# A two-layer encoder trunk: normed chunks one group earlier, and three kinds of steps on another engine

## The chip, the cores and the metric

The kernel runs on one core of a Trainium2 chip. Its time is the device time of one launch in microseconds (us), from the first instruction to the last with the little that lies around them. Beside the times there is one profiled execution, which records every instruction of each engine: PE (TensorE: matmuls; PEld is its weight load), DVE (VectorE), ACT (ScalarE), POOL (GpSimd) and SP (SyncE, which issues the DMAs). The granted clock of TensorE is recorded too, as a share of full speed.

## What is computed

A trunk of two layers over 272 rows: 256 tokens and 16 learned meta rows, 2048 features wide, in float32. For each layer, cut to what matters:

```
proj = h @ w_in                                   # 2048 x 6176: GLA q,k,v,r, decay; NA q,k,v
g    = log_sigmoid(decay @ w_up + b_up) / 16      # gates of the gated linear attention (GLA)
# GLA, both directions: scores[t,s] = sum_d q[t,d] k[s,d] exp(b[t,d] - b[s,d]),  b = cumsum(g)
# NA: each token attends to a window of its 64-wide grid, and to the meta rows
h = layer_norm(alpha*h + concat(gla*silu(r), na) @ w_out) * ln1_w + ln1_b
h = layer_norm(alpha*h + square(relu(h @ w_ff1)) @ w_ff2) * ln2_w + ln2_b
```

`w_ff1` is 2048 x 8192. The meta rows are dropped at the end, so that the last layer works on 256 rows from its output projection on (n = 256; elsewhere n = 272).

## The kernel before

**Matmuls.** Activations lie transposed: 16 chunks (DC) of 128 features x n rows. A float32 product is made of three float32r products: each operand is split into a high part (rounded to float32r) and a low part (what is left), and high·high, high·low and low·high are summed. A weight tile is 128 x 1024 numbers, that is eight blocks of 128 x 128. `weights` (L118) loads it (`raw`, a DMA that SP issues), ScalarE makes the high part `wh` (L126) and VectorE the low part `wl` (L127); three tiles of each are in flight. `three` (L130) does one block: with n = 256 the high weight part meets both halves of the activation in one matmul of 512 columns (L135) and the low part makes a second (L136); otherwise there are three matmuls (L139 to L141).

Output columns come in groups of 512, eight weight tiles each. `by_m` (L169) makes a group's four 128-column outputs one after the other, each in a PSUM bank of its own, from two weight tiles. `by_k` (L152) keeps four banks open and takes the activation chunks in pairs, a weight tile for each pair, so that it can begin before all chunks are there (L165).

**What sets the order.** The rest of the work (evictions, attention, norms) is written as generators in two queues, `fg` and `bg`. `pump` (L102) steps them between weight tiles by the credits it is given, `drain` empties them. The framework's planner then orders the instructions of each engine by priority and by costs of its own; a step is issued behind the last `wl` made (`issue_after(self.wl)` in `step`). Each engine works through its own list in order.

**Behind a norm.** `ln_norm` (L796) makes mean and variance. `ln_all` (L816) then goes through the chunks in pairs: VectorE subtracts the mean and multiplies with 1/sigma over two chunks at once (`ln_wide`, L833), and GpSimd applies gain and bias to each of the two (L823). `renew` (L835) splits a normed chunk anew into high and low (L186, L187). TensorE can't wait for this. So the first two groups behind a norm use chunks that aren't normed, with gain multiplied in and two extra columns at their end (n+2), and `fix` (L848) corrects the outputs after: it copies the two columns' sums (`wb`, L857), and takes mean and 1/sigma into account (`fx`, L858 and L859). Group 0 is by_m with `pump=(1, NORMS)`, NORMS = 0.4, which steps `ln_all` now and then; group 1 is by_k with `renew` called at each pair, which makes `ln_all` go on where it has not yet done the chunk. From group 2 on the chunks are normed ones. There are three such places: FF1 in either layer, and in layer 1 the first two projection groups (`win[0]`, `win[1]`).

**Gate differences.** GLA's decays between two positions are made level by level: at each of eight levels (`operands`, L424) the running sums of gates `be` (forward and backward direction) are subtracted from one of their own entries in the middle of each block, for the query and the key side: four GpSimd subtractions (L437), then exp on ScalarE (L442) and the product with q and k on VectorE (L443). Four heads, two layers: 64 levels.

**Residual parts.** In `mixed` (L260, the add is L266) GpSimd adds the high and low part of each old chunk to get the residual back, 16 chunks in each layer.

Of the kernel before, what the change touches and what calls it, by code (L numbers as in the profile page):

```python
# [34 lines left out]
GLA_R, GLA_NA, NORMS = 1.3, 1.1, 0.4  # L35
# [11 lines left out]
class Trunk:  # L47
    def __init__(self, ctx, tc, ins, out):
        self.ctx, self.tc, self.nc = ctx, tc, tc.nc
        self.i, self.out = ins, out  # L50
        self.bg, self.fg, self.credit, self.fcredit = deque(), deque(), 0, 0
        self.x = [None] * DC
        pool = lambda name, **k: ctx.enter_context(tc.tile_pool(name=name, **k))
        self.cp = pool("const", bufs=1)
        self.xp = pool("xhl", bufs=1)
        self.yp = pool("yhl", bufs=1)
        self.wp = pool("wst", bufs=3)
        self.jp = pool("jn", bufs=1)
        self.pm = pool("pm", bufs=4, space=PSUM)
        self.pb = pool("pb", bufs=4, space=PSUM)  # L60
# [57 lines left out]
    def weights(self, ap, parts=1):  # L118
        nc = self.nc
        size = ap.shape[-1]  # L120
        raw, wh, wl = (self.wp.tile([P, WB], d, name=nm, tag=nm)[:, :size]
                       for nm, d in (("raw", F32), ("wh", F32R), ("wl", F32R)))
        for p in range(parts):
            c = slice(p * size // parts, (p + 1) * size // parts)
            nc.sync.dma_start(raw[:, c], ap[:, c])
            nc.scalar.copy(wh[:, c], raw[:, c])  # L126
            self.wl = nc.vector.tensor_tensor(wl[:, c], raw[:, c], wh[:, c].bitcast(F32), ALU.subtract).ins  # L127
        return wh, wl

# [39 lines left out]
    def by_m(self, w, acts, ns, evict, pump=(0, 0), apart=False):  # L169
# [3 lines left out]
        for m, n in enumerate(ns):  # L173
            ps = self.pm.tile([P, 512], F32, name="mm", tag="mm")
            for k in range(nk):
                if k % 8 == 0:
                    wh, wl = self.weights(w[m * per + k // 8])
                self.three(ps, wh, wl, (k % 8) * P, acts[k], n, k == 0, k == nk - 1)
                if k % 8 == 7 and k < nk - 1:
                    self.pump(*pump)  # L180
            parts = [ps[:, :T], ps[:, T:]] if n == T else [ps[:, :n]]
            evict(m, parts if apart else self.whole(parts))
            self.pump(*pump)
# [16 lines left out]
    def layer(self, l):  # L200
# [5 lines left out]
        with ExitStack() as actx:  # L206
# [10 lines left out]
            if l:  # L217
                self.by_m(win[0], self.x, [L + 2] * 4, lambda m, ps: self.fixed(self.ev_k, m, ps), pump=(1, NORMS))
                ps = self.by_k(win[1], self.x, L + 2, self.renew)
                self.renew(DC)  # L220
                for m in range(4):
                    self.fixed(self.ev_v, m, ps[m])
# [7 lines left out]
            with ExitStack() as ectx:  # L230
# [3 lines left out]
                if l == 0:  # L234
                    self.by_m(win[1], self.x, [L] * 4, self.ev_v, pump=(1, 0))
                self.by_m(win[2], self.x, [n] * 4, self.ev_q, pump=(1, 0))
# [23 lines left out]
    def mixed(self, k):  # L260
# [3 lines left out]
        for c in (k, k + 1):  # L264
            h, lo = (t[:, :self.n].bitcast(F32) for t in self.x[c])
            self.nc.gpsimd.tensor_tensor(self.acc[:, c, :self.n], h, lo, ALU.add)  # L266
# [74 lines left out]
    def ev_v(self, c, ps, **how):  # L341
        pool, bufs = (self.l3, 3) if how else (self.ep, 2)
        vt = pool.tile([P, L], F32, name="ft", tag="ft", bufs=bufs)
        self.nc.scalar.activation(vt, ps, AF.Identity, **how)
# [70 lines left out]
    def gla_head(self, h):  # L415
# [8 lines left out]
        def operands(lv):  # L424
# [8 lines left out]
            v = lambda a: a[:, :w].rearrange("p (b h) -> p b h", h=B)  # L433
            f, e, tq, tk = v(bf), v(eb), v(t[:, 0, :]), v(t[:, 1, :])
            mf = f[:, :, hb - 1:hb].to_broadcast([P, nb, hb])
            me = e[:, :, hb:hb + 1].to_broadcast([P, nb, hb])
            tt = lambda o, x, y: nc.gpsimd.tensor_tensor(o, x, y, ALU.subtract)  # L437
            tt(tq[:, :, hb:], f[:, :, hb:], mf)
            tt(tq[:, :, :hb], me, e[:, :, :hb])
            tt(tk[:, :, :hb], mf, f[:, :, :hb])  # L440
            tt(tk[:, :, hb:], e[:, :, hb:], me)
# [202 lines left out]
    def tail(self, ps):  # L644
# [3 lines left out]
        with tc.tile_pool(name="u", bufs=1, reuse_waits="tile") as up:  # L648
# [6 lines left out]
            for half in range(2):  # L655
                u = [self.pair(self.yp, "y", k) if k < DC else self.pair(up, "u", k) for k in range(2 * DC)]

                def ev_f(k, ps, **how):
                    h, lo = u[k]
                    t = self.l3.tile([P, L], F32, name="ft", tag="ft")[:, :n]  # L660
                    if how or n > T:
                        nc.scalar.activation(t, ps, AF.Relu, **how)
                        nc.vector.tensor_tensor(t, t, t, ALU.mult)
# [4 lines left out]
                for g in range(8):  # L668
# [3 lines left out]
                    elif g:  # L672
                        ps = self.by_k(w, self.x, n + 2, self.renew)
                        self.renew(DC)
                        for m in range(4):
                            self.fixed(ev_f, 4 + m, ps[m])
                        self.step(self.fg, 2)
                    else:
                        self.by_m(w, self.x, [n + 2] * 4, lambda m, ps: self.fixed(ev_f, m, ps), pump=(1, NORMS))
# [116 lines left out]
    def ln_norm(self, which, l, n):  # L796
# [14 lines left out]
        self.norm = dict(mu=mu, rs=rs, last=end, n=n, ready=0, gb=[self.affine(l, which, k) for k in range(DC)])  # L811
# [4 lines left out]
    def ln_all(self):  # L816
        nc, acc, n = self.nc, self.acc, self.norm["n"]
        for k in range(0, DC, 2):
            self.ln_wide(k, 2, 0)
            self.ln_wide(k, 2, 1)  # L820
            for c in (k, k + 1):
                a, (gain, bias) = acc[:, c, :n], self.norm["gb"][c]
                nc.gpsimd.tensor_scalar(a, a, gain, bias, ALU.mult, ALU.add)  # L823
# [11 lines left out]
    def renew(self, k):  # L835
# [3 lines left out]
        for c in (k - 2, k - 1) if k else ():  # L839
# [3 lines left out]
            self.split(self.acc[:, c, :n], h[:, :n], lo[:, :n])  # L843

# [133 lines left out]
```

## Time and profile before

| | us |
|---|---|
| median of 3 runs | 2456.98 (2456.32 to 2459.82) |
| the profiled execution | 2457.63 |
| its span, first instruction to last | 2455.8 |
| TensorE busy | 2413.3 |
| VectorE busy | 1579.7 |
| ScalarE busy | 1177.6 |
| GpSimd busy | 334.8 |

How to read the rows below. A group of instructions has its line, engine and operation, the tiles it writes and reads, its shape and the number of instructions; behind the bar the busy time, the mean length in ns, and the idle time of its engine just before them with what ended it. A row of the timeline has start, length, engine, line, and in brackets the idle time ahead of it and its releaser. Recorded lengths of neighbours overlap, since an engine begins an instruction before the last one has ended: what an instruction takes of its engine's time is the distance from start to start. The waits give total, number and longest. A line can be that of a helper that many callers use.

### The profile page before, as it was taken

To read this page: it belongs to the slowest core of one execution; us is meant where nothing else is said; L and a number is where in the kernel's file an instruction comes from. 1 tells how busy PE (TensorE), PEld (TensorE's weight loads), DVE (VectorE), ACT (ScalarE), POOL (GpSimd) and SP (SyncE) were. 2 spreads that over 40 slices of the span, in tenths; PEclk is the share of its full clock that TensorE was granted. 3 is DMA by queue.
4 is the path that set the end of the run, shared out by engine and by line. 5 is a ranking of instruction groups with operands and counts; after the bars stand their busy time and mean duration, and the time that the engine had idled before them with its cause. 6 is when DMAs were issued, how large, how long until landed. Compare 5 with 4: busy or idle time off the path is not lost.

```text
span 2455.8 us, 43396 instructions
## 1 busy us (share of the span) xinstructions
PE 2413.3 (98%) x17388; PEld 2261.6 (92%) x17388; DVE 1579.7 (64%) x2481; ACT 1177.6 (48%) x1938; POOL 334.8 (14%) x503
## 2 busy tenths in 40 slices
PE   9999999999999999999999999999899999999997
PEld 9999899999999999999998888888888888888886
DVE  6687677785544455546578777768866555666655
ACT  6555555554433344444446555555544333444443
POOL 1164340030000000000023444310300000000000
PEclk9999999999999999999999999999999999999998
DMA  7544444555555555555555444446555656566654
GB/s 238 163 134 145 139 135 153 175 158 178 172 177 176 172 177 175 173 177 174 173 184 165 146 142 149 135 152 198 157 187 188 189 189 188 184 187 188 188 189 129
DMA packets 118362, 417.26 MB, mean 170 GB/s; under 512 B 13388, under 2 KB 16460, under 8 KB 118160
## 3 DMA queue, kind: packets, MB, share of 16 engines
q1 hardware_dynamic: 118160, 414.49, 53.9%
q8 instruction: 136, 2.23, 0.4%
q14 instruction: 66, 0.54, 0.1%
HBM read 412.34 MB, written 2.10 MB: 169 GB/s over the span
## 4 chain that ended last, share of the span: by engine, by line
PE 93%; DVE 2%; POOL 2%; issue 1%; ACT 1%; DMA 0%; SPq 0%; ACTq 0%; POOLq 0%; DVEq 0%
PE mm L135 22%; PE mm L139 17%; PE mm L141 17%; PE mm L140 17%; PE mm L136 11%; PE mm L165 5%; POOL lev L437 2%; DVE wl L127 1%; PE bg L472 1%; DVE acc L833 1%; PE bg L622 0%; POOL acc L823 0%; PE bg L574 0%; PE bg L624 0%; PE bg L301 0%
## 5 line engine op out<-in xcount | busy, mean ns | idle before, releaser
L127 DVE TENSOR_TENSOR wl<-raw,wh 128x1024 fp32r<-128x1024 f32 (+1 forms) x772 | 948.3, 1229 | 645.1 <-ACT wh L126 638.2
L126 ACT CAST wh<-raw 128x1024 fp32r<-128x1024 f32 (+1 forms) x772 | 805.7, 1044 | 945.3 <-PE mm L140 417.9
L139 PE MATMUL mm<-x,wh 128*128 128x272 f32 (+2 forms) x2112 | 615.7, 292 | 4.0 <-DVE wb L857 4.0
L141 PE MATMUL mm<-x,wl 128*128 128x272 f32 (+2 forms) x2112 | 611.3, 289 | 2.5 <-DVE wl L127 2.5
L140 PE MATMUL mm<-x,wh 128*128 128x272 f32 (+2 forms) x2112 | 610.7, 289 | 0.0
L135 PE MATMUL mm<-x,wh 128*128 128x512 f32 x1216 | 434.7, 399 | 6.5 <-DVE fx L858 6.5
L139 PEld LDWEIGHTS mm<-x,wh 128*128 128x128 f32 x2112 | 402.1, 190 | 8.6 <-issue 5.5
L141 PEld LDWEIGHTS mm<-x,wl 128*128 128x128 f32 x2112 | 399.3, 189 | 2.9 <-DVE wl L127 2.8
L140 PEld LDWEIGHTS mm<-x,wh 128*128 128x128 f32 x2112 | 398.6, 189 | 0.0
L136 PE MATMUL mm<-x,wl 128*128 128x256 f32 x1216 | 343.9, 283 | 1.9 <-DVE wl L127 1.9
L135 PEld LDWEIGHTS mm<-x,wh 128*128 128x128 f32 x1216 | 230.7, 190 | 61.9 <-issue 7.0
L135 PE MATMUL mm<-y,wh 128*128 128x512 f32 x704 | 248.3, 393 | 0.3 <-ACT wh L126 0.3
L136 PEld LDWEIGHTS mm<-x,wl 128*128 128x128 f32 x1216 | 230.7, 190 | 2.5 <-DVE wl L127 2.2
L141 PE MATMUL mm<-y,wl 128*128 128x272 f32 x704 | 203.1, 288 | 0.0
L139 PE MATMUL mm<-y,wh 128*128 128x272 f32 x704 | 203.1, 288 | 0.0
L140 PE MATMUL mm<-y,wh 128*128 128x272 f32 x704 | 202.7, 288 | 0.0
L136 PE MATMUL mm<-y,wl 128*128 128x256 f32 x704 | 197.7, 281 | 1.0 <-DVE wl L127 1.0
L135 PE MATMUL mm<-u,wh 128*128 128x512 f32 x512 | 180.6, 393 | 0.0
L437 POOL TENSOR_TENSOR lev<-be 128x128 f32<-128x128 f32 (+1 forms) x256 | 151.9, 623 | 152.0 <-PE bg L472 64.9
L135 PEld LDWEIGHTS mm<-y,wh 128*128 128x128 f32 x704 | 131.9, 187 | 30.9 <-ACT wh L126 0.7
L141 PE MATMUL mm<-u,wl 128*128 128x272 f32 x512 | 147.7, 289 | 0.0
L139 PE MATMUL mm<-u,wh 128*128 128x272 f32 x512 | 147.7, 288 | 0.0
(241 smaller groups left out, 3334.4 us busy)
## 6 DMA issues: line engine op xcount, KB each, us to landing
raw<-in_wff SPq DMA_DIRECT2D x512, 512.0 KB, 3.5
raw<-in_win SPq DMA_DIRECT2D x190, 512.0 KB, 3.6
raw<-in_wout SPq DMA_DIRECT2D x64, 512.0 KB, 3.6
nb<-in_nab SPq DMA_DIRECT2D x16, 352.0 KB, 3.8
out<-acc SPq DMA_DIRECT2D x8, 256.0 KB, 2.2
xraw<-in_xT SPq DMA_DIRECT2D x7, 272.0 KB, 4.5
wraw<-in_wup SPq DMA_DIRECT2D x2, 392.0 KB
raw<-in_win SPq DMA_DIRECT2D x4, 128.0 KB, 3.0
```

The source lines that it names most:

```text
L126: nc.scalar.copy(wh[:, c], raw[:, c])
L127: self.wl = nc.vector.tensor_tensor(wl[:, c], raw[:, c], wh[:, c].bitcast(F32), ALU.subtract).ins
L135: mm(ps, lhsT=wh[:, c:c + P], rhs=x.both[:, :, :T], start=first, stop=False)
L136: mm(ps[:, T:], lhsT=wl[:, c:c + P], rhs=xh[:, :T], start=False, stop=last)
L139: mm(o, lhsT=wh[:, c:c + P], rhs=xh[:, :n], start=first, stop=False)
L140: mm(o, lhsT=wh[:, c:c + P], rhs=xl[:, :n], start=False, stop=False)
L141: mm(o, lhsT=wl[:, c:c + P], rhs=xh[:, :n], start=False, stop=last)
L165: self.nc.tensor.matmul(ps[m][:, :n], lhsT=parts[p][0][:, c:c + P], rhs=acts[j][parts[p][1]][:, :n], start=j + p == 0, stop=j == nk - 1 an ...
L437: tt = lambda o, x, y: nc.gpsimd.tensor_tensor(o, x, y, ALU.subtract)
L472: nc.tensor.matmul(ps[b * 64:b * 64 + 64, s * 64:s * 64 + 64], lhsT=k[:, c:c + 64], rhs=q[:, r:r + 64], start=True, stop=True)
L833: return self.nc.vector.tensor_tensor(v, v, by[:, None, :].to_broadcast([P, m, n]), alu)
```

## The change

Group 1 behind each of the three norms takes normed chunks (n columns instead of n+2) and needs no correction. For that `ln_all` is stepped at every pump of group 0 (NORMS 1.0), `by_m(renew=True)` splits the first six chunks (LEAD) in the middle of group 0's last output, and `normed` keeps by_k six chunks ahead. `ln_all` gives the gain and bias of every other chunk to ScalarE. `fetch` makes the first weight tile of group 2 ahead of the queue's drain or step, evictions of group 1 are plain (`ev_v` a copy in the early pool with four buffers; `later` queues those of FF1), and squares of corrected or some uncorrected FF1 outputs move between engines. The gate differences become two VectorE subtractions for each level, both directions in one, through hand-made access patterns. The residual adds go to VectorE.

```diff
--- before.py
+++ after.py
@@ -32,7 +32,8 @@
 EPS = 1e-5
 TAU = 16.0
 NEG = -1e30
-GLA_R, GLA_NA, NORMS = 1.3, 1.1, 0.4
+GLA_R, GLA_NA, NORMS = 1.3, 1.1, 1.0
+LEAD = 6
 
 
 class Pair(tuple):
@@ -50,6 +51,7 @@
         self.i, self.out = ins, out
         self.bg, self.fg, self.credit, self.fcredit = deque(), deque(), 0, 0
         self.x = [None] * DC
+        self.next = deque()
         pool = lambda name, **k: ctx.enter_context(tc.tile_pool(name=name, **k))
         self.cp = pool("const", bufs=1)
         self.xp = pool("xhl", bufs=1)
@@ -116,6 +118,8 @@
 
 
     def weights(self, ap, parts=1):
+        if self.next:
+            return self.next.popleft()
         nc = self.nc
         size = ap.shape[-1]
         raw, wh, wl = (self.wp.tile([P, WB], d, name=nm, tag=nm)[:, :size]
@@ -126,6 +130,10 @@
             nc.scalar.copy(wh[:, c], raw[:, c])
             self.wl = nc.vector.tensor_tensor(wl[:, c], raw[:, c], wh[:, c].bitcast(F32), ALU.subtract).ins
         return wh, wl
+
+    def fetch(self, ap):
+
+        self.next.append(self.weights(ap))
 
     def three(self, ps, wh, wl, c, x, n, first, last):
 
@@ -166,7 +174,7 @@
                                       start=j + p == 0, stop=j == nk - 1 and p == 2)
         return [p[:, :n] for p in ps]
 
-    def by_m(self, w, acts, ns, evict, pump=(0, 0), apart=False):
+    def by_m(self, w, acts, ns, evict, pump=(0, 0), apart=False, renew=False):
 
         nk = len(acts)
         per = nk // 8
@@ -178,6 +186,8 @@
                 self.three(ps, wh, wl, (k % 8) * P, acts[k], n, k == 0, k == nk - 1)
                 if k % 8 == 7 and k < nk - 1:
                     self.pump(*pump)
+                if renew and m == len(ns) - 1 and k == 8:
+                    self.renew(LEAD)
             parts = [ps[:, :T], ps[:, T:]] if n == T else [ps[:, :n]]
             evict(m, parts if apart else self.whole(parts))
             self.pump(*pump)
@@ -215,11 +225,10 @@
             nc.gpsimd.memset(self.VS.bitcast(F32), 0.0)
             self.y, self.gate, self.done = [None] * DC, {}, set()
             if l:
-                self.by_m(win[0], self.x, [L + 2] * 4, lambda m, ps: self.fixed(self.ev_k, m, ps), pump=(1, NORMS))
-                ps = self.by_k(win[1], self.x, L + 2, self.renew)
-                self.renew(DC)
-                for m in range(4):
-                    self.fixed(self.ev_v, m, ps[m])
+                self.by_m(win[0], self.x, [L + 2] * 4, lambda m, ps: self.fixed(self.ev_k, m, ps), pump=(1, NORMS),
+                          renew=True)
+                first = self.by_k(win[1], self.x, L, self.normed)
+                self.fetch(win[2][0])
                 self.drain()
                 self.lctx.close()
             else:
@@ -233,6 +242,9 @@
                 self.fg.append(self.gates())
                 if l == 0:
                     self.by_m(win[1], self.x, [L] * 4, self.ev_v, pump=(1, 0))
+                else:
+                    for m, ps in enumerate(first):
+                        self.ev_v(m, ps)
                 self.by_m(win[2], self.x, [n] * 4, self.ev_q, pump=(1, 0))
                 self.by_m(win[3], self.x, [L] * 4, lambda m, ps: self.ev_v(4 + m, ps), pump=(1, 0))
                 self.drain()
@@ -263,7 +275,7 @@
             self.step(self.fg, 1)
         for c in (k, k + 1):
             h, lo = (t[:, :self.n].bitcast(F32) for t in self.x[c])
-            self.nc.gpsimd.tensor_tensor(self.acc[:, c, :self.n], h, lo, ALU.add)
+            self.nc.vector.tensor_tensor(self.acc[:, c, :self.n], h, lo, ALU.add)
 
     def load_x(self, k):
         nc = self.nc
@@ -338,10 +350,9 @@
     def ev_k(self, m, ps, **how):
         self.nc.scalar.activation(self.qk[m][:, 1, :], ps, AF.Identity, **how)
 
-    def ev_v(self, c, ps, **how):
-        pool, bufs = (self.l3, 3) if how else (self.ep, 2)
-        vt = pool.tile([P, L], F32, name="ft", tag="ft", bufs=bufs)
-        self.nc.scalar.activation(vt, ps, AF.Identity, **how)
+    def ev_v(self, c, ps):
+        vt = self.ep.tile([P, L], F32, name="ft", tag="ft", bufs=4)
+        self.nc.scalar.copy(vt, ps)
         self.fg.append(self.v_rows(c, vt))
 
     def v_rows(self, c, vt):
@@ -430,15 +441,12 @@
             B, hb = 1 << lv, 1 << (lv - 1)
             nb = w // B
             t = level()
-            v = lambda a: a[:, :w].rearrange("p (b h) -> p b h", h=B)
-            f, e, tq, tk = v(bf), v(eb), v(t[:, 0, :]), v(t[:, 1, :])
-            mf = f[:, :, hb - 1:hb].to_broadcast([P, nb, hb])
-            me = e[:, :, hb:hb + 1].to_broadcast([P, nb, hb])
-            tt = lambda o, x, y: nc.gpsimd.tensor_tensor(o, x, y, ALU.subtract)
-            tt(tq[:, :, hb:], f[:, :, hb:], mf)
-            tt(tq[:, :, :hb], me, e[:, :, :hb])
-            tt(tk[:, :, :hb], mf, f[:, :, :hb])
-            tt(tk[:, :, hb:], e[:, :, hb:], me)
+            v = lambda a: a[:, :, :w].rearrange("p d (b h) -> p d b h", h=B)
+            b, o = v(be), v(t)
+            mid = bass.AP(be.tensor, be.offset + hb - 1, [b.ap[0], [L + 2, 2], [B, nb], [0, hb]])
+            back = bass.AP(be.tensor, be.offset + hb + L + 1, [b.ap[0], [-L - 2, 2], [B, nb], [0, hb]])
+            nc.vector.tensor_tensor(o[:, :, :, hb:], b[:, :, :, hb:], mid, ALU.subtract)
+            nc.vector.tensor_tensor(o[:, :, :, :hb], back, b[:, ::-1, :, :hb], ALU.subtract)
             nc.scalar.activation(t[:, :, :w], t[:, :, :w], AF.Exp, scale=1 / TAU)
             nc.vector.tensor_tensor(t[:, :, :w], t[:, :, :w], qk[:, :, :w], ALU.mult)
             return t[:, 0, :], t[:, 1, :]
@@ -658,8 +666,11 @@
                 def ev_f(k, ps, **how):
                     h, lo = u[k]
                     t = self.l3.tile([P, L], F32, name="ft", tag="ft")[:, :n]
-                    if how or n > T:
+                    if how:
                         nc.scalar.activation(t, ps, AF.Relu, **how)
+                        nc.scalar.activation(t, t, AF.Square)
+                    elif n > T or not half and 3 < k < 8:
+                        nc.scalar.activation(t, ps, AF.Relu)
                         nc.vector.tensor_tensor(t, t, t, ALU.mult)
                     else:
                         nc.vector.scalar_tensor_tensor(t, ps, 0.0, ps, ALU.max, ALU.mult)
@@ -670,13 +681,13 @@
                     if half or g > 1:
                         self.by_m(w, self.x, [n] * 4, lambda m, ps: ev_f(4 * g + m, ps), pump=(1, 0))
                     elif g:
-                        ps = self.by_k(w, self.x, n + 2, self.renew)
-                        self.renew(DC)
-                        for m in range(4):
-                            self.fixed(ev_f, 4 + m, ps[m])
-                        self.step(self.fg, 2)
+                        ps = self.by_k(w, self.x, n, self.normed)
+                        self.fetch(self.i["wff1"][l, 2, 0])
+                        self.fg.extend(self.later(ev_f, 4 + m, ps[m]) for m in range(4))
+                        self.step(self.fg, 1)
                     else:
-                        self.by_m(w, self.x, [n + 2] * 4, lambda m, ps: self.fixed(ev_f, m, ps), pump=(1, NORMS))
+                        self.by_m(w, self.x, [n + 2] * 4, lambda m, ps: self.fixed(ev_f, m, ps), pump=(1, NORMS),
+                                  renew=True)
 
                 def ev_2(m, ps, g):
                     k = 4 * g + m
@@ -808,7 +819,7 @@
         nc.scalar.copy(mu, p1)
         nc.vector.tensor_tensor(var, p2, tn, ALU.subtract)
         end = self.newton(rs, var, self.eps, tn)
-        self.norm = dict(mu=mu, rs=rs, last=end, n=n, ready=0, gb=[self.affine(l, which, k) for k in range(DC)])
+        self.norm = dict(mu=mu, rs=rs, last=end, n=n, ready=0, new=0, gb=[self.affine(l, which, k) for k in range(DC)])
         if not which or l < DEPTH - 1:
             self.bg.append(self.ln_all())
         yield
@@ -820,7 +831,10 @@
             self.ln_wide(k, 2, 1)
             for c in (k, k + 1):
                 a, (gain, bias) = acc[:, c, :n], self.norm["gb"][c]
-                nc.gpsimd.tensor_scalar(a, a, gain, bias, ALU.mult, ALU.add)
+                if c % 2:
+                    nc.gpsimd.tensor_scalar(a, a, gain, bias, ALU.mult, ALU.add)
+                else:
+                    nc.scalar.activation(a, a, AF.Identity, bias=bias, scale=gain)
             self.norm["ready"] = k + 2
             yield
 
@@ -832,15 +846,25 @@
         by, alu = ((f["mu"], ALU.subtract), (f["rs"], ALU.mult))[op]
         return self.nc.vector.tensor_tensor(v, v, by[:, None, :].to_broadcast([P, m, n]), alu)
 
-    def renew(self, k):
+    def normed(self, k):
+
+        self.pump(1, 0)
+        self.renew(min(DC, k + LEAD))
+
+    def renew(self, end):
 
         f = self.norm
         n = f["n"]
-        for c in (k - 2, k - 1) if k else ():
+        for c in range(f["new"], end):
             while f["ready"] <= c:
                 self.step(self.bg, 1)
             h, lo = self.x[c]
             self.split(self.acc[:, c, :n], h[:, :n], lo[:, :n])
+        f["new"] = end
+
+    def later(self, evict, m, ps):
+        evict(m, ps)
+        yield
 
     def fixed(self, evict, m, ps):
         self.fg.append(self.fix(evict, m, ps))
```

## The prediction

> **What bounds the kernel now.** First the page: busy time of each engine and the costliest group that the change removes.
>
> ```profile
> span 2455.8 us, 43396 instructions
> PE 2413.3 (98%) x17388; PEld 2261.6 (92%) x17388; DVE 1579.7 (64%) x2481; ACT 1177.6 (48%) x1938; POOL 334.8 (14%) x503
> ...
> L437 POOL TENSOR_TENSOR lev<-be 128x128 f32<-128x128 f32 (+1 forms) x256 | 151.9, 623 | 152.0 <-PE bg L472 64.9 <-DVE be L326 23.8 <-ACT gt L315 22.4
> ```
>
> TensorE is the bound, at 98%. Nothing in the change takes whole matmuls from it, so what can be won is its idle time, and matmuls that ran at a low clock. Second, TensorE's waits: total, times, longest.
>
> ```profile
> PE mm L135 <- DVE fx L858: 6.5, 2, 5.2
> ...
> PE mm L139 <- DVE wb L857: 4.0, 1, 4.0
> PE mm L136 <- DVE wl L127: 2.9, 2, 1.9
> PE mm L141 <- DVE wl L127: 2.5, 1, 2.5
> PE mm L165 <- DVE wl L127: 1.5, 2, 1.2
> ...
> PE bg L353 <- ACT ft L344: 0.8, 1, 0.8
> ```
>
> Third, its timeline around two of these, start and length in us first, the idle time before the instruction in brackets.
>
> ```profile
> 524.02 0.29 PE L165 MATMUL mm<-x,wh 128*128 128x274 f32 x1
> 528.27 0.44 PE L139 MATMUL mm<-x,wh 128*128 128x272 f32 x1 [3.96 <-DVE wb L857]
> ...
> 531.69 0.35 PE L139 MATMUL mm<-x,wh 128*128 128x272 f32 x1
> 531.88 0.29 PE L140 MATMUL mm<-x,wh 128*128 128x272 f32 x1
> 532.00 0.29 PE L141 MATMUL mm<-x,wl 128*128 128x272 f32 x1
> ...
> 1383.94 0.39 PE L136 MATMUL mm<-x,wl 128*128 128x256 f32 x1 [1.90 <-DVE wl L127]
> ...
> 1439.97 0.60 PE L141 MATMUL mm<-x,wl 128*128 128x272 f32 x1 [2.53 <-DVE wl L127]
> ```
>
> Fourth, stretches around the waits and in the attention: start and end; length, then busy time (and instructions) of PE, weight load, DVE, ACT, POOL; granted clock; DMA share; GB/s.
>
> ```profile
> 160.00:190.00 30.00, 30.00 (x274) 28.22 (x274) 25.31 (x43) 14.37 (x25) 22.32 (x34) 1.00 0.40 124
> 524.00:534.00 10.00, 6.04 (x36) 5.84 (x35) 8.45 (x21) 5.91 (x11) 2.97 (x4) 0.83 0.32 106
> 1300.00:1310.00 10.00, 7.88 (x55) 6.76 (x53) 9.12 (x23) 6.21 (x12) 5.18 (x5) 1.00 0.56 165
> 1380.00:1390.00 10.00, 8.10 (x49) 6.32 (x48) 7.57 (x13) 5.78 (x11) 8.15 (x11) 0.83 0.37 125
> 1410.00:1440.00 30.00, 27.47 (x219) 23.67 (x217) 24.92 (x43) 16.68 (x31) 20.86 (x37) 1.00 0.38 121
> 1436.00:1446.00 10.00, 7.47 (x42) 6.54 (x42) 7.53 (x12) 5.78 (x11) 4.54 (x11) 0.83 0.47 150
> 1756.00:1766.00 10.00, 5.00 (x21) 4.37 (x22) 8.45 (x21) 5.44 (x10) 3.75 (x4) 0.83 0.30 106
> ```
>
> A wait of 1.90 us or more brings the clock down for a while: 15 matmuls from 528.27 to 531.69 start 0.228 us apart instead of 0.127, so 1.5 us lost. With the wider tiles of the last layer I take 1.7. After the wait of 1.35 at 1305 the clock stayed at 1.00. So a wait of about 2 us costs 3.7, one of 1.3 just itself: a threshold between the two, which I shall need.
>
> **The change, part by part. (a) Group 1 takes normed chunks.** There are three places: FF1 of each layer and the second projection group of layer 1. Why TensorE waits there now is in GpSimd's timeline and in the chain's step for that group.
>
> ```profile
> 518.10 2.78 POOL L823 TENSOR_SCALAR acc<-acc,vec 128x272 f32<-128x272 f32 x2 [1.19 <-DVE acc L833]
> 522.07 2.78 POOL L823 TENSOR_SCALAR acc<-acc,vec 128x272 f32<-128x272 f32 x2 [1.19 <-DVE acc L833]
> ...
> 1279.38 24.44 PE mm L165 x192
> ```
>
> A pair of chunks is made every 3.97 us, TensorE eats one every 24.44/8 = 3.05 us, and by the group's end it has outrun the chunks that group 2 needs. The waits at the three ends are 4.0 + 6.5 + 1.2 (the longest of L165's on wl) + 0.8 = 12.5 us, and two clock drops (0.83 at 524 and at 1756) add 1.5 + 1.7: 15.7 us.
>
> After the change half of the gain-and-bias steps run on ScalarE, and the chunks are begun in group 0: the loop at the end goes, and with it those 15.7. What is late next is on VectorE. Group 0's sixth weight tile now has eight wide norm steps ahead of it in VectorE's order; before it had one.
>
> ```profile
> 482.14 1.23 DVE L127 TENSOR_TENSOR wl<-raw,wh 128x1024 fp32r<-128x1024 f32 x1 [0.84 <-ACT wh L126]
> 483.28 0.43 DVE L809 TENSOR_TENSOR var<-bg,tn 128x272 f32<-128x272 f32 x1
> 483.63 0.49 DVE L858 SCALAR_TENSOR_TENSOR fx<-mu,wb,mm 128x272 f32<-128x272 f32 x1
> 484.04 0.72 DVE L833 TENSOR_TENSOR acc<-acc,mu 128x544 f32<-128x544 f32 x1
> ...
> 485.72 1.23 DVE L127 TENSOR_TENSOR wl<-raw,wh 128x1024 fp32r<-128x1024 f32 x1
> ...
> 490.83 0.29 PE L141 MATMUL mm<-x,wl 128*128 128x274 f32 x1
> ```
>
> The last row is the first use of that tile (written at 485.72). From start to start, var takes 0.36, a correction step 0.41, a wide step 0.64. Behind 483.28 then stand var 0.36, eight wide steps 5.1, three Newton steps 1.2, two tiles' corrections 1.6 and a split 0.4: the tile starts at 492.0 and is ready at 493.2, 2.4 late, of which 0.3 is covered by matmuls that the new order puts ahead of it: 2.1. By-k's first tile stands behind six splits (2.2) and the last wide steps: again about 2.1. The same count for the other two places gives 1.7 + 0.3 and 2.1 + 2.3. Sum 10.6 us, in four waits at the threshold. I let two of them drop the clock (3.4): 14.0 instead of 15.7, **−1.7**. Bounds: none of it arises (−15.7), or all waits a third longer and four drops (14 + 6.8, so +5.1).
>
> Two columns less in three groups: 24.44/192 = 0.127 us a matmul, 2/274 of it is 0.9 ns, over 576 matmuls **−0.5**. The first tile of the next group fetched ahead, squares and gain steps on ScalarE (24 steps of about 0.5 us in three places) and later evictions cost nothing while ScalarE has 41% free in such a stretch (5.91 of 10 at 524); without that cover they would delay a weight tile's copy by the same 0.5 each. The early load of the gate weights moves ahead of weight loads in SP's queue: DMA is 40% busy or less in that kind of stretch, so nothing.
>
> **(b) Gate differences to VectorE.**
>
> ```profile
> L437 POOL TENSOR_TENSOR lev<-be 128x128 f32<-128x128 f32 (+1 forms) x27 | 18.6, 719 | 6.5 <-PE bg L472 4.2 <-PE bg L475 2.3
> ...
> L127 DVE TENSOR_TENSOR wl<-raw,wh 128x1024 fp32r<-128x1024 f32 x7 | 9.5, 1355 | 0.0
> ...
> L127 DVE TENSOR_TENSOR wl<-raw,wh 128x1024 fp32r<-128x1024 f32 x56 | 68.6, 1225 | 62.2 <-ACT wh L126 62.2
> ```
>
> (The first two from 160 to 190, the last from 530 to 700.) A level loses four GpSimd steps of 623 ns and gains two VectorE steps of 256 or 272 elements. No row shows them; between a 128-element step's 0.2 and the wide step's 0.64 I take var's 0.36, of the same size: 0.72 a level, 46 us over 64 levels. Weight subtractions beside a busy GpSimd took 1355 ns, without it 1225: some of this is given back. [...]
>
> In layer 1 VectorE waits in order for the levels, with weight tiles behind:
>
> ```profile
> 1437.13 0.42 DVE L455 TENSOR_TENSOR lev<-lev,qk 128x256 f32<-128x256 f32 x1 [2.36 <-ACT lev L454]
> ...
> 1438.60 1.32 DVE L127 TENSOR_TENSOR wl<-raw,wh 128x1024 fp32r<-128x1024 f32 x1
> ```
>
> That is the wait at 1439.97. Now: 2.9 + 2.5 idle, less 1.0 of it elsewhere, but with 2 × 1.7 for the clock, 7.8 in all. After: 7 levels × 0.72 = 5.0 on top of 24.92 busy of 30 makes VectorE full, and I leave half, 1.8 idle and one drop: 3.5, **−4.3** (bounds −7.8 and 0). In layer 0 no wait stands there now: 25.31 + 6.75 × 0.72 = 30.2 of 30, less 7 × 0.13 = 0.9 and as much for the other steps: 28.4. It just fits; **+1.0** for a wait or two (bounds 0 and the rival below).
>
> **(c) Residual adds to VectorE.** The two stretches where they run now, in the view of the stretches:
>
> ```profile
> 353.00:380.00 27.00, 27.00 (x220) 25.57 (x219) 19.83 (x43) 16.70 (x57) 16.70 (x22) 1.00 0.42 133
> 1592.00:1608.00 16.00, 16.00 (x119) 14.82 (x118) 12.81 (x21) 9.26 (x26) 15.70 (x20) 1.00 0.48 151
> ```
>
> 32 × 0.36 = 11.5 us, 5.8 a layer. VectorE is idle 7.2 of 27 us in the one and 3.2 of 16 in the other, where a part is given back: GpSimd's work of 16 us a stretch, which slows VectorE as above, is gone (by 130 ns on each of 4 to 7 weight tiles, and on the rest in proportion). TensorE never waits there. **0**: the idle time covers it; without that cover 5.8 − 3.2 = 2.6 in layer 1 would reach the end (bounds −0.5 and +4.3, that with a drop of the clock).
>
> Sum: −1.7 − 0.5 − 4.3 + 1.0 + 0 = −5.5, against the profiled run's 2457.63 (span 2455.8): 2452.1. That run lies 0.65 over the median 2456.98, so **2451.5**.
>
> **The rivals.** *Whole gain* (0.23): TensorE never meets the new waits because matmuls put ahead cover them. For it: the order has twelve such places. Against: VectorE is at 8.45 to 9.12 of 10 in all three stretches. From the forecast's sum up to −15.7 − 0.5 − 4.3 + 1.0 = −19.5 on the median: 2437.5 to 2448.
> [...] Without the three drops that I charge (3.4 + 1.7) the time would be 2446.4; 0.05 of the 0.23.
>
> *Nothing gained in the attention* (0.22): the change doesn't do what it says there, as VectorE, with the differences on it, delays the tile as much as the wait did. For it: it becomes full. −4.3 falls away: 2455.8, within 0.2% (4.9 us, about what a measurement can tell).
>
> *Slower* (0.25): VectorE works in order, and in layer 0 the 28.4 of 30 is an estimate; at 0.5 us instead of 0.36 a difference step, 30.3 of 30 is needed. Then each stretch like 160 to 190 (six of them) ends with a tile 2 us late and a clock drop, 3.7 each in place of the 1.0. Three bring 2450.5 to 2462, from which it counts as slower; four to 2465, six to 2473. Against: the contention falls away for every VectorE step, not just for those counted.
>
> **How the numbers follow.** Forecast 0.30 (2448 to 2452), whole gain 0.23, within 0.2% 0.22 (2452 to 2462), slower 0.25 (2462 to 2475). The range 2440 to 2466 leaves out some 0.05 below and 0.13 above. Faster is the first two, less a little for the forecast's edge, which lies near the bound: 0.52; same 0.23; slower 0.25.
>
> **What would show it.** (a) right: no wait on wb, fx or on the loop at the ends of the three by-k groups, but waits of about 2 us on the weights' low part in the middle of group 0 and at by-k's start. (b) right: difference steps of 0.36 to 0.45 us on VectorE, weight subtractions near 1225 ns from 160 to 190, one wait left of the two in layer 1. (c) right: no wait near the residual adds. Wrong if waits on the low part turn up in layer 0's attention with a clock under 1.00 there, or if group 0's waits are absent.

## The result

The changed kernel takes **2472.59 us** (median; 2470.65 to 2473.42). The kernel before had 2457.64 beside it. The ratio is 1.0059, 95% interval 1.0041 to 1.0076: 15 us slower. The forecast was 2451.5; the range, 2440 to 2466, doesn't hold the time.

The page of the kernel after: TensorE is as bound as before, GpSimd has lost 200 us, VectorE has gained 22.

```profile
span 2468.9 us, 42981 instructions
PE 2419.8 (98%) x17388; PEld 2264.6 (92%) x17388; DVE 1601.3 (65%) x2597; ACT 1190.3 (48%) x1970; POOL 134.0 (5%) x191
```

TensorE's waits after (total, times, longest):

```profile
PE mm L149 <- DVE wl L131: 10.8, 8, 2.1
PE mm L173 <- ACT wh L130: 4.8, 2, 4.3
PE bg L475 <- DVE lev L451: 4.5, 2, 2.7
PE mm L173 <- DVE wl L131: 2.6, 3, 1.2
PE mm L173 <- DVE fx L882: 2.4, 2, 1.3
PE mm L143 <- ACT wh L130: 1.9, 2, 1.6
PE mm L144 <- DVE wl L131: 1.7, 3, 1.0
```

The long waits on `wb` and `fx` at the ends of the by-k groups (4.0 and 5.2) are gone, as meant (the 4.3 for `wh` is the kernel's start, 4.8 before). In their place are many shorter waits for weight tiles and, new, for the attention's level products (L451).

Where the time went is read by taking the start of the same weight matmul, counted from the first (16,000 in each kernel), in both profiled runs: stretch by stretch, in us.

| stretch (weight matmuls) | before | after | |
|---|---|---|---|
| start to the end of layer 0's attention (0 to 2112) | 339.8 | 349.1 | +9.3 |
| the three places behind the norms (2112 to 3600, 9312 to 9840, 11880 to 12240) | 342.0 | 340.4 | −1.6 |
| layer 1's attention (9840 to 11520) | 313.4 | 318.6 | +5.2 |
| all else | 1437.2 | 1437.2 | 0.0 |

So the places behind the norms gained 1.6 us, close to the 2.2 that were forecast. (Across the experiments below, the four kernels with the old groups took 342.0 to 343.6 us there, and the eight with the new ones and the same NORMS and LEAD 338.9 to 341.3.) The attention, forecast to gain 3.3 in all (+1.0 in layer 0, −4.3 in layer 1), lost 14.5. (The profiled run, 2470.65, is 2 us under the median.)

One of the new waits, in the timelines of the kernel after, engine by engine:

```profile
137.09 0.41 DVE L449 TENSOR_TENSOR lev<-be 128x256 f32<-128x256 f32 x1
137.42 1.22 DVE L131 TENSOR_TENSOR wl<-raw,wh 128x1024 fp32r<-128x1024 f32 x1
141.45 0.69 DVE L451 TENSOR_TENSOR lev<-lev,qk 128x512 f32<-128x512 f32 x1 [2.82 <-ACT lev L450]
...
135.92 1.06 ACT L130 CAST wh<-raw 128x1024 fp32r<-128x1024 f32 x1
140.25 0.66 ACT L462 ACTIVATE lev<-lev 128x544 f32<-128x544 f32 x1 [3.26 <-POOL lev L461]
140.81 0.61 ACT L450 ACTIVATE lev<-lev 128x512 f32<-128x512 f32 x1
...
136.25 1.15 POOL L458 TENSOR_SCALAR lev<-be 128x256 f32<-128x256 f32 x1
...
139.07 1.14 POOL L461 TENSOR_SCALAR lev<-be 128x256 f32<-128x256 f32 x1
...
142.29 0.57 PE L475 MATMUL bg<-lev 128*128 128x128 f32 x3 [1.83 <-DVE lev L451]
```

Read it from the bottom. TensorE waits 1.83 us for the product of the last level. VectorE waits 2.82 for that level's exp (L450). The exp's input was ready at 137.5 (L449 in the first row), but on ScalarE the exp of the *cross-half* step (L462) stands ahead of it, and that one waits 3.26 us for four GpSimd instructions (L458 to L461; `across` in the code, the step that follows the last level). In the kernel before the same three engines did this:

```profile
134.66 0.63 ACT L442 ACTIVATE lev<-lev 128x512 f32<-128x512 f32 x1 [0.70 <-POOL lev L437]
135.20 1.04 ACT L126 CAST wh<-raw 128x1024 fp32r<-128x1024 f32 x1
...
140.24 0.66 ACT L454 ACTIVATE lev<-lev 128x544 f32<-128x544 f32 x1 [3.44 <-POOL lev L453]
140.81 1.03 ACT L126 CAST wh<-raw 128x1024 fp32r<-128x1024 f32 x1
```

ScalarE waited just as long (3.44), but behind the last level's exp, so that VectorE had its product. In the written-out order of ScalarE's instructions all eight heads before have eight level exps and then the cross-half one; after, in the first six heads, seven and then the cross-half one, with the eighth behind it. While GpSimd made the differences too, the cross-half step came after them in GpSimd's own order. With GpSimd empty of differences, the planner put its exp early; that this is the planner's reason is an inference.

### The profile page after: what moved, and what is told of

Its sections match the earlier page's. It is cut to its first block, busy times and chain, and to the rows that moved or that the text cites. A ratio compares the mean times of both kernels' runs of the same rounds, so it can differ in the third digit from the quotient of the medians.

```text
span 2468.9 us, 42981 instructions
## 1 busy us (share of the span) xinstructions
PE 2419.8 (98%) x17388; PEld 2264.6 (92%) x17388; DVE 1601.3 (65%) x2597; ACT 1190.3 (48%) x1970; POOL 134.0 (5%) x191
## 4 chain that ended last, share of the span: by engine, by line
PE 91%; DVE 4%; issue 2%; POOL 1%; ACT 1%; DMA 0%; SPq 0%; ACTq 0%; DVEq 0%; POOLq 0%
PE mm L143 22%; PE mm L147 16%; PE mm L149 16%; PE mm L148 16%; PE mm L144 11%; PE mm L173 6%; DVE acc L847 1%; DVE wl L131 1%; PE bg L480 1%; PE bg L632 0%; PE bg L630 0%; PE bg L582 0%; PE bg L313 0%; ACT wh L130 0%; POOL lev L461 0%
## 5 line engine op out<-in xcount | busy, mean ns | idle before, releaser
L147 PE MATMUL mm<-u,wh 128*128 128x272 f32 x512 | 147.7, 288 | 0.0
L148 PE MATMUL mm<-u,wh 128*128 128x272 f32 x512 | 147.5, 288 | 0.0
```

The source lines that it names most:

```text
L147: mm(o, lhsT=wh[:, c:c + P], rhs=xh[:, :n], start=first, stop=False)
L148: mm(o, lhsT=wh[:, c:c + P], rhs=xl[:, :n], start=False, stop=False)
```

## Experiments

The names used: **A**, the loss comes from this order on ScalarE (**A2**: and from GpSimd's slow cross-half step wherever it stands); **B**, from VectorE being too full, the prediction's own rival; **C**, from the new groups; **D**, the waits in group 0 come from the norm's wide steps ahead of a weight tile (**D2**: those steps only move). Each kernel ran beside the kernel before; kernels of different sets are compared through their ratios to it, since it moved between 2456.6 and 2458.2.

**Differences back on GpSimd** in the changed kernel (the four GpSimd subtractions of the kernel before, in place of the two on VectorE):

> The changed kernel with the gate differences back on GpSimd (four subtractions a level); groups behind the norms and residual adds as changed. In the changed kernel's profile the attention stretches lost 9.3 us in layer 0 and 5.2 in layer 1, and the three places behind the norms gained 0.1, 0.7 and 0.8. Theory A (the attention loses by an order on ScalarE: the exp of the cross-half step, fed by GpSimd, stands ahead of the last level's exp) and theory B (VectorE is too full with the differences on it) both expect the attention as before: 2456 us, between 2454 and 2458. Theory C (the loss comes from the new group order or the residual adds, which shift the attention's start) expects 2465 us or more.

2457.44 us, ratio to before 0.9998 (0.9988 to 1.0007). The whole loss is gone: C, as the only cause, falls.

**Only the differences on VectorE**, in the kernel before (the same edit the other way):

> The kernel before with one part of the change: the gate differences as two VectorE subtractions a level. Theories A and B: the attention's whole loss is here, 2457.6 + 14.5 = 2472 us, between 2469 and 2475. Theory C: 2460 us or less.

2468.07 us, ratio 1.0039 (1.0024 to 1.0054). By the stretches above, layer 0 up to its attention's end takes 350.0 (+10.2), layer 1's attention 313.3 (−0.1). So the part alone makes two thirds of the loss, all in layer 0; layer 1's loss needs the new groups too, which this experiment had not been expected to show (miss by 4 us). The exps on ScalarE stand in the changed kernel's order here too, in both layers.

**The order on ScalarE restored** in the changed kernel:

```diff
-            nc.scalar.activation(t[:, :, :w], t[:, :, :w], AF.Exp, scale=1 / TAU)
+            self.exp = nc.scalar.activation(t[:, :, :w], t[:, :, :w], AF.Exp, scale=1 / TAU).ins
...
-            nc.scalar.activation(t, t, AF.Exp, scale=1 / TAU)
+            with self.tc.issue_after(self.exp):
+                nc.scalar.activation(t, t, AF.Exp, scale=1 / TAU)
```

> The changed kernel with one more edit: the exp of the cross-half step is queued on ScalarE behind the exp of the last level in every head, as it was before the change. Nothing else is edited; VectorE keeps the differences. Theory A: six heads stop waiting; TensorE's waits of 1.83, 0.79, 1.75, 1.36 and 2.70 us (the last with a clock drop of 1.7) go, so 2472.6 - 10.1 = 2462.5 us, between 2459 and 2465, and VectorE's idle times of 2.8 us ahead of the last level's product are gone. Theory B: VectorE's load is unchanged, so 2470 us or more.

2462.88 us, ratio 1.0021 (1.0011 to 1.0030): some 10 of the 15 us come back (4.7 over its own kernel before, against 15.0) by an edit of order alone. In the attention stretches TensorE and GpSimd keep their order, on VectorE two steps change places, and on ScalarE only the exps and one copy move. A is shown. It isn't all: 5.4 us are left to the kernel with the differences on GpSimd, which ran beside it. Of four remaining waits of TensorE, those near 262 and 1402 us still have ScalarE waiting for the cross-half step ahead of them, now behind the last exp, and a weight copy and VectorE's next steps stand behind it (those near 186 and 1383 us don't):

```profile
254.05 0.63 ACT L450 ACTIVATE lev<-lev 128x512 f32<-128x512 f32 x1 [0.57 <-DVE lev L449]
257.12 0.66 ACT L463 ACTIVATE lev<-lev 128x544 f32<-128x544 f32 x1 [2.44 <-POOL lev L461]
...
258.09 0.17 DVE L379 TENSOR_SCALAR nq<-mm 128x16 f32<-128x16 f32 x1 [2.33 <-ACT nq L377]
```

**Only the groups changed** (differences and residual adds back on GpSimd):

> The changed kernel with gate differences and residual adds back on GpSimd: only the groups behind the norms are changed. Both theories: 2456 us (2457.6 less 1.6, what the three places gained), 2453 to 2458. The difference to the kernel with the adds on VectorE shows what the adds are worth: forecast 0, not over 1 us.

2457.42 us, ratio 0.9997 (0.9988 to 1.0007). Against the first experiment the residual adds are worth 0.0 us (each ratio is known to 0.1%, some 2 us). The three places take 340.6 us, 1.4 less than before; in the whole time that can't be told from nothing.

**Cross-half step on VectorE too** (order restored; `ts = nc.vector.tensor_scalar` in `across`):

> The changed kernel with the exp order restored, and the cross-half step's four GpSimd instructions (3.3 us a head and more) given to VectorE as well. The kernel with the order alone took 2462.9, 5.4 over the one with the differences on GpSimd (2457.4). Theory A2 (what is left of the loss is the same wait for GpSimd's cross-half step, 2.0 to 2.3 us of VectorE's idle time in two of four looks): 2457 to 2459 us. Theory B (what is left is VectorE's load): the load grows by some 0.8 us a head, so 2463 to 2465.

2460.78 us, ratio 1.0014 (1.0005 to 1.0024). Against the 1.0021 of the last but one that is 0.07%, under 2 us and within the intervals, not the 4 to 6 us of A2, which this doesn't bear out.

**More load on VectorE alone**, in the kernel before; in each level

```diff
+            u = g2.tile([P, 2], F32, name="extra", tag="extra", bufs=1)
+            for d in range(2):
+                nc.vector.tensor_reduce(u[:, d:d + 1], be[:, d, :w], mybir.AxisListType.X, ALU.max)
```

> The kernel before, with two more VectorE instructions in each level that nothing needs: the maximum over each of the level's two gate rows (256 or 272 elements), written to a scratch. GpSimd keeps the differences, so only VectorE's load grows, by about as much as the differences (0.7 to 0.8 us a level, some 48 us). Theory B: 2458.2 + 5 = 2463 us or more. Theory A2: within 2 us of before, 2457 to 2460.

2481.39 us, ratio 1.0100 (1.0083 to 1.0117). 128 steps of 409 ns (52 us by their recorded lengths, 42 from start to start) on an engine that is 64% busy, 76% in layer 0's attention, cost 24.8 us, five times the least that theory B expected. But not only the load changed: the planner also wrote the rest in another order, TensorE's matmuls too (in 28 places up to the end of layer 0's attention), so that the load's own part of the 24.8 is open.

**Only the cross-half step moved**, in the kernel before:

> The kernel before, with only the cross-half step's four instructions on VectorE instead of GpSimd. ScalarE waits 21.8 us for that step in all, and VectorE 17.4 behind it; TensorE's wait of 2.53 us at 1439.97 with its clock drop stands behind the third head's. Theory A2: that wait goes, 2458.2 - 4.2 = 2454 us, between 2452 and 2456. Theory B: some 0.8 us a head more on VectorE, 2458 to 2460.

2455.24 us, ratio 0.9995 (0.9986 to 1.0004): layer 1's attention takes 309.7 instead of 313.4, as A2 had it, and layer 0 takes 341.4 instead of 339.8. In sum it can't be told from no change; 2454 had been expected.

**Differences on GpSimd, cross-half step on VectorE**, in the changed kernel:

> The changed kernel with the gate differences back on GpSimd and the cross-half step on VectorE: the parts that gained, and the one removed wait. 2457.4 - 4.2 = 2453 us by theory A2, 2457 to 2460 by theory B.

2453.90 us, ratio 0.9988 (0.9979 to 0.9997). Less than both kernels, by 2.7 us (before: 2456.59).

**Half of the differences**: with order and cross-half step as two runs above, the second subtraction of each level goes to GpSimd (`nc.gpsimd.tensor_tensor(o[:, :, :, :hb], ...)`):

> The changed kernel with the exp order restored and the cross-half step on VectorE (2460.8), and of the two subtractions a level one more step: the second goes back to GpSimd, so half of the differences' VectorE time (some 26 us) is gone. If what is left of the loss is VectorE's load, the time lies between 2460.8 and 2453.9 (all differences on GpSimd), about 2457. If it isn't the load but the differences' place in the order, it stays at 2460 or more.

2450.40 us, ratio 0.9969 (0.9957 to 0.9981). Not between the ends but under both: 0.9988 with all on GpSimd, 0.9969 with half, 1.0014 with all on VectorE. The first half on VectorE gains 0.19% (4.7 us), the second costs 0.45% (11 us). Neither is a pure move: GpSimd makes its half in one instruction a level where the kernel with all on GpSimd has four, and TensorE's order differs between the three kernels.

**The norm's steps spread out**, from the kernel of 2453.9: `NORMS = 0.5`; `NORMS = 0.4, LEAD = 2`; `NORMS = 0.7, LEAD = 4`.

> The kernel of 2453.9 (differences on GpSimd, cross-half step on VectorE) with the norm stepped half as often in group 0 (NORMS 0.5 instead of 1.0): two wide steps instead of eight stand ahead of group 0's sixth weight tile. Theory D (the waits of 1.89, 1.55 and 1.98 us there come from those steps, as predicted): they go, 5.4 us, 2448.5, between 2447 and 2451. Rival D2 (the norm's VectorE work is only moved, and TensorE waits for it at by-k's start or end): 2453 to 2457.

2447.26 us, ratio 0.9959 (0.9944 to 0.9974). The waits in group 0 are gone. D is shown.

> The same kernel with NORMS 0.4 (as before the change) and two chunks split ahead instead of six (LEAD 2). Theory D: no wait in group 0, and by-k's start waits less behind the splits (now 1.1 + 0.7, 1.2, 1.2 + 0.7 us), so 2446 to 2450. Rival D2: chunks come too late, by-k waits inside for them, 2453 or more.

2452.54 us, ratio 0.9979 (0.9970 to 0.9989). D2 is right for this one, though the time lies just under its 2453: by-k waits inside for chunks that are split too late,

```profile
PE mm L173 <- ACT x L196: 9.9, 8, 2.8
```

> The same kernel with NORMS 0.7 and LEAD 4: three wide steps ahead of the sixth weight tile. Theory D: between the last two, 2447 to 2451. Rival D2: 2453 or more.

2447.18 us, ratio 0.9958 (0.9941 to 0.9975). The three places take 333.2 us instead of 342.0 before and 340.4 after: this is what the idea of the change is worth in these stretches, 8.8 us, if its steps don't hold up group 0's weight tiles.

**What gained, together:**

> What gained, together: one difference step a level on each of VectorE and GpSimd, the cross-half step on VectorE behind the last level's exp, and the norm stepped at NORMS 0.7 with LEAD 4. If the two gains are of separate places they add: 2450.4 - (2453.9 - 2447.2) = 2443.7, between 2442 and 2446. If one wait only hides the other: 2447 or more.

2442.93 us, ratio 0.9942 (0.9926 to 0.9959): the two add up. This version is 14 us faster than the kernel before and, by the ratios, 29 than the changed one.

**The same extra load with GpSimd nearly idle** (the two maxima a level on top of the kernel of 2460.8):

> The kernel with all differences and the cross-half step on VectorE and the exp order restored (2460.8), with the same two maxima a level added that cost the kernel before 24.8 us (2456.6 to 2481.4); GpSimd is nearly idle here. If a full VectorE is what costs, 52 us more of it costs at least as much here, where it is fuller: 2485 us or more. If the 24.8 came from VectorE and GpSimd slowing each other, it costs clearly less here: 2470 or less.

2496.26 us, ratio 1.0157 (1.0141 to 1.0172): the load costs 1.43% here (35 us) against 1.00% (24.8 us). It isn't the two engines slowing each other: GpSimd is nearly idle here (15.86 of 227 us and 13.85 of 188 in the rows below). TensorE's largest waits but for the one at the start are for VectorE, many and none over 2.1 us:

```profile
PE mm L149 <- DVE wl L131: 13.0, 16, 2.1
PE bg L484 <- DVE lev L454: 10.0, 11, 1.5
PE mm L144 <- DVE wl L131: 6.6, 8, 1.5
```

Is it VectorE's load, then? The attention stretches, 113 to 340 and 1372 to 1560, first of this kernel, then of the one with the same load in the kernel before (2481.39), then of the one of 2442.93 (columns as in the prediction: length, PE, weight load, VectorE, ScalarE, GpSimd, clock):

```profile
113.00:340.00 227.00, 214.48 (x1741) 196.50 (x1739) 194.78 (x459) 114.80 (x250) 15.86 (x35) 0.97 0.40 123
1372.00:1560.00 188.00, 174.43 (x1223) 149.00 (x1222) 159.06 (x341) 100.21 (x206) 13.85 (x30) 0.97 0.43 132
```

```profile
113.00:340.00 227.00, 218.44 (x1808) 199.73 (x1808) 182.52 (x396) 118.31 (x258) 98.41 (x175) 0.99 0.42 128
1372.00:1560.00 188.00, 177.21 (x1269) 154.28 (x1268) 152.01 (x294) 102.74 (x214) 80.45 (x140) 0.96 0.45 135
```

```profile
113.00:340.00 227.00, 226.80 (x1914) 210.06 (x1914) 184.55 (x401) 126.73 (x281) 41.32 (x67) 1.00 0.47 140
1372.00:1560.00 188.00, 186.69 (x1404) 164.34 (x1404) 161.44 (x311) 109.89 (x231) 39.32 (x63) 1.00 0.51 152
```

VectorE isn't 100% busy in any, and its busy share doesn't decide. In layer 0 TensorE idles 8.6 us with VectorE 80% busy (182.52 of 227), and 0.2 with 81% (184.55). In layer 1 it idles 13.6 us at 85% (159.06 of 188), and 1.3 at 86% (161.44). So it isn't shown that a full VectorE is what costs; where its steps stand in the order is the open rival. In both added-load kernels the planner has written TensorE's matmuls in another order as well; what the load alone costs was not separated.

## Why the prediction was wrong

**(a) Group 1: right.** The waits at the ends of the by-k groups went, and on VectorE the sixth weight tile of group 0 and by-k's start became late, where the prediction had put them. Group 0: 2.1, 1.7, 2.1 us were forecast; 1.90, 1.55 and 2.07 came. By-k's start: 2.1, 0.3, 2.3 were forecast; 1.80, 1.18 and 1.96 came. The sum is 10.5 against 10.6; that it is so close is partly luck, since the misses at by-k's starts (−0.3, +0.9, −0.3) cancel. Three drops of the clock came with these waits, where two had been charged. (By-k's start waits in part, 2.4 us in two waits, for a correction, `fx`, that frees a bank, and only in part behind the splits that were named.) The three places gained 1.6 us, forecast 2.2. The DMA share, put at 40% or less, is 0.56 in the prediction's own row from 1300; no wait of TensorE for a DMA came of it.

**(c) Residual adds: right.** 0 forecast, 0.0 measured, within some 2 us.

**(b) Differences: the step that failed.** Layer 0's term, +1.0, came out as +9.3, and layer 1's, −4.3, as +5.2. Its prices were right: a step takes 0.34 us from start to start (0.36 forecast), and weight subtractions beside them came back from 1355 to 1241 ns, as these rows from 160 to 190 of the kernel after show.

```profile
L131 DVE TENSOR_TENSOR wl<-raw,wh 128x1024 fp32r<-128x1024 f32 x7 | 8.7, 1241 | 1.2 <-ACT wh L130 1.2
...
L448 DVE TENSOR_TENSOR lev<-be 128x272 f32<-128x272 f32 (+1 forms) x7 | 2.8, 400 | 0.0
...
160.00:190.00 30.00, 28.98 (x259) 27.05 (x258) 26.90 (x56) 16.18 (x28) 5.47 (x6) 1.00 0.37 113
```

VectorE has 26.9 of 30 us there; "it just fits; +1.0" was an estimate of 28.4. It fitted, and TensorE lost 1.02 us in that very stretch, as the "wait or two" had it. Two things were wrong. First, the sum of busy times said that there was room, and nothing was said of *order*: whose exp stands ahead of whose on ScalarE. That made some 10 us of 15, in places where neither VectorE nor GpSimd was full (8.01 and 1.48 of 10 us from 140). The prediction looked at what GpSimd no longer delayed, but not at what GpSimd still fed: its cross-half step, whose price was in the trace before (ScalarE's wait for L453 in the view of L453, and for L461 after):

```profile
  ACT lev L454: 21.8, 7
  ACT lev L462: 23.4, 8
```

The wait is about as long after as before, 23.4 against 21.8 us; only what stands behind it has changed. Second, in layer 1 the forecast took −4.3 for two waits, 1.90 and 2.53 us, each with a drop of the clock, that GpSimd's differences were held to cause. With the differences alone on VectorE both are gone, as forecast, yet the stretch took only 0.1 us less: a new wait of 2.70 us with a drop stands behind the cross-half exp, and there are shorter ones, 4.9 us in all. With the groups changed too, one of 1.58 us with a drop was added, and the stretch took 5.2 more. With just the cross-half step moved, the second wait shrank to 0.31 us and the first stayed at 1.90; the stretch took 3.7 less. So the second wait was the cross-half step's, as the row quoted for it (2.36 us for L454, the cross-half exp) said. The forecast counted what would go, and put what would come at 1.8 us and one drop.

**The rivals.** "Slower" (0.25; 2462 to 2475) holds the time, and its place, layer 0's attention, is where most was lost. Its mechanism is half right. TensorE waits in five places there (1.83, 1.02, 0.79, 1.75 and 1.36 us), but without a drop of the clock, while the rival had priced one with each. With ScalarE's order restored the first and the last are gone, 0.79 and 1.75 are down to 0.32 and 1.27, and only the 1.02 stays: VectorE was late first because it waited for ScalarE. What was left once the order was mended (5 to 7 us) goes with the differences back on GpSimd, but whether it is a full VectorE, as the rival put it, or the planner's placement of the steps is not shown.

**The clock.** (a) needed a threshold between 1.35 and 1.90 us, and these runs show none in the length of a wait. In the kernel after, waits of 1.83 and 1.75 us kept the clock at 1.00, and those of 1.90, 2.70 and 2.07 brought it to 0.83 (in the stretches of 10 us behind each); but so did one of 1.58 us at 1386.65 and, at by-k's third start, two of 1.27 and 0.69. The last section has more on these. For the 0.05, that none of the three drops charged would come (2446.4), no run shows a ground: the kernel after has five drops to 0.50 ahead of its last 15 us.

```profile
140.00:150.00 10.00, 8.17 (x62) 7.40 (x61) 8.01 (x13) 6.52 (x12) 1.48 (x2) 1.00 0.45 134
265.00:275.00 10.00, 9.46 (x69) 8.71 (x70) 8.01 (x20) 6.82 (x19) 1.07 (x2) 1.00 0.64 211
501.00:511.00 10.00, 9.09 (x59) 9.09 (x60) 8.71 (x16) 6.60 (x16) 8.89 (x5) 0.83 0.47 126
1403.00:1413.00 10.00, 9.66 (x47) 7.83 (x48) 8.77 (x15) 5.03 (x11) 0.41 (x1) 0.83 0.35 107
1738.00:1748.00 10.00, 9.42 (x66) 9.42 (x67) 8.84 (x18) 6.86 (x18) 8.31 (x5) 0.83 0.49 145
```

## What to carry to other kernels

When steps leave one engine, read the whole written-out order of every in-order engine that they feed, and ask which of the steps that stay behind will now be placed earlier: here a wait cost by what stood behind it, not by its length (ScalarE's for the cross-half step: 21.8 us before, 23.4 after). The busy share of VectorE didn't tell how much room it had, with TensorE in need of a `wl` from it for every weight tile: the kernels with some 42 us of extra VectorE steps took 25 and 35 us more, while at the same busy share (80 and 81% in layer 0's attention, 85 and 86% in layer 1's) another kernel lost next to nothing (0.2 and 1.3 us of TensorE's time there). And before a group of steps is moved whole from a slow engine to a full one, try half: it beat both ends here (2450.40 us against 2453.90 and 2460.78).

## What was not expected of the hardware

In these runs the length of a wait doesn't tell whether TensorE's clock drops. A wait of 2.54 us in the kernel with the differences back on GpSimd kept it at 1.00, and one of 1.58 in the kernel after halved it. In the trace of the kernel after the clock falls to 0.50 at 502.82, 1386.87, 1403.94, 1738.44 and 1752.10 (and once more in the last 15 us), each of the five times for 3.41 us; from the first to the last of them are 1249.28 us, 366 times 3.413, and the four distances are 259, 5, 98 and 4 times that. In the trace of the kernel before it falls at 528.41, 1385.15, 1439.76 and 1760.62, again for 3.41 us, and once more in the last 15; the distances of the four are 251, 16 and 94 times 3.413. The rows below are stretches of this length, those of the kernel after at such distances from its drops (for the three rows of the other kernel that is not shown here). First the 2.54 us (1439.02 to 1441.56), which lie in two of its rows, then the 1.58, the 2.70 and the 1.27 and 0.69 in the kernel after (length, then PE's busy time; the clock is the third number from the end):

```profile
1437.06:1440.48 3.42, 1.96 (x16) 1.74 (x15) 1.70 (x6) 2.39 (x6) 2.83 (x8) 1.00 0.33 135
1440.48:1443.89 3.41, 2.33 (x18) 2.33 (x19) 3.41 (x5) 1.81 (x3) 1.29 (x1) 1.00 0.34 119
1443.89:1447.30 3.41, 3.41 (x20) 2.56 (x20) 3.02 (x3) 1.58 (x3) 2.06 (x4) 1.00 0.85 211
...
1383.46:1386.87 3.41, 1.83 (x15) 1.11 (x13) 3.13 (x9) 2.22 (x5) 0.00 (x0) 1.00 0.22 87
1386.87:1390.29 3.42, 3.42 (x17) 2.68 (x17) 3.36 (x7) 1.35 (x4) 0.97 (x1) 0.50 0.30 99
1400.53:1403.94 3.41, 0.71 (x6) 0.64 (x6) 1.44 (x4) 2.41 (x4) 0.73 (x1) 1.00 0.50 154
1403.94:1407.35 3.41, 3.41 (x13) 2.58 (x12) 2.78 (x5) 0.37 (x1) 0.00 (x0) 0.50 0.19 18
1748.69:1752.10 3.41, 1.45 (x10) 1.19 (x10) 3.41 (x8) 3.41 (x8) 1.62 (x1) 1.00 0.02 7
1752.10:1755.51 3.41, 3.41 (x18) 3.41 (x18) 3.41 (x7) 1.80 (x6) 0.00 (x0) 0.50 0.71 186
```

The 2.54 us leave 1.46 and 1.08 idle in two neighbouring stretches, and the clock stays; 1.58, 2.70 and 1.96 idle in one stretch each have 0.50 in the next. That the idle time within one stretch is what counts is the author's reading of these cases. In the traces of the kernels before and after, counted this way and without their first and last 15 us, the other six drops came behind stretches with 1.90 to 3.41 us idle, and no stretch with more than 1.65 kept the clock. But no sharp bound is shown: 1.65 idle kept it at 1.00 twice (263.89 to 267.30 after, 1303.23 to 1306.65 before), where 1.58 halved it. A drop takes some 1.7 us, by an estimate from the 3.41 us at 0.50.
